# Feed-forward layers' last projections on one core: four weight blocks asked for one to two pairs sooner, all token parts in double tiles, neighbourhood steps regrouped

## The chip, the cores and the metric

The kernel runs on one core of a Trainium2 chip: TensorE (PE, matmuls), VectorE (DVE), ScalarE (ACT), GpSimd (POOL), SyncE (SP, which issues most loads) and 16 DMA engines. The metric is the device time of one execution in microseconds (us), the lower the better.

## The reference

One layer for 512 tokens of width 1024 in float32: a feed-forward layer (FFN1), a mixer of two attention branches, and a second feed-forward layer (FFN2), each between RMS norms.

```python
def _swiglu(x, w_gate, w_up, w_down):
    return (jax.nn.silu(x @ w_gate) * (x @ w_up)) @ w_down      # w_gate, w_up: 1024 x 2816, w_down: 2816 x 1024
...
f = _swiglu(_rmsnorm(x, ffn1_pre_g[l]), ffn1_w_gate[l], ffn1_w_up[l], ffn1_w_down[l])
x = x + 0.5 * _rmsnorm(f, ffn1_post_g[l])
h = _rmsnorm(x, mix_pre_g[l])
proj = h @ w_in[l]                                              # 1024 x 5888
...
ya = _neighbourhood_attention(qa, ka, va, na_rpb[l]) @ w_branch_a[l]   # 8 heads of 64, an 8 x 16 neighbourhood
yb = _dilated_mixture(qb, kb, vb, slopes) @ w_branch_b[l]
merged = jax.nn.sigmoid(gate_a) * ya + jax.nn.sigmoid(gate_b) * yb
x = x + _rmsnorm(merged @ w_out[l], mix_post_g[l])
# and f, x once more with the weights of ffn2
```

## The kernel before

**Numbers in two parts.** Every float32 operand is split into a high part (a cast by ACT, L116) and a low part (a subtraction by DVE, L117); a product is three matmuls into one bank: high by high, high by low, low by high (`mm3`, L207 to L209). PE takes both parts of both operands, so a product waits for ACT and, for its third matmul at the latest, for DVE's low parts.

**Seven products.** The matrices of the feed-forward layers are cut into two by two blocks and multiplied with seven products instead of eight (numbered 1 to 7), which need sums and differences of blocks. Sums of weight blocks are made by accumulating DMAs, issued by POOL (a second block is added on top of a loaded one while it is moved), or by DVE; differences of token parts (`v`) by DVE.

**The last projection** (`down`, class `Blocks`). The hidden features stand in units; its weight blocks are 128 x 1024 each, `((i, j), d)` for i, j in 0, 1 and d = 0 to 4, and one narrower row `EXTRA`. `order` is the list of (product, d) that PE runs through: (2,0), (2,1), then product 1 for all d, 5, 6, the rest of 2, 7, then 3 and 4. `prep` makes what one of them needs: the token part (`tokens`, its split into `a` or `pair`) and the weight block (`rows`, its split into `w`), `AHEAD` = 6 places before PE's `run`. Product 1 takes block (0,0) as loaded; product 5 takes it after block (0,1) was added by DMA (`t1`), product 6 that plus block (1,1) (`t2`: by DMA for d = 2 to 4 (L724), by DVE at L774 for d = 0 and 1).

**Places in memory.** A unit is 128 x 512 (`unit`, 38 of them, shared by nearly everything). `ta`, `tb`, `ba`, `bb` are larger places, each for two blocks, that were parts of the normalised tokens `hn`; they come free only when PE has read `hn` for the last time. Of the blocks (0,0) and (1,1), d = 0 to 3 go to `ta`, `tb` and `ba`, `bb`, and d = 4 into units, in two halves (`rows`, L731). A token part's high and low part are either two units (`a`) or one double tile (`pair`, 8 of them, `twin`); `o.paired` says which parts get a double tile: from the ninth on every third.

**When loads are asked for.** During the last pairs of the first projections (`seven`, 20 pairs of block columns) the function `get(j)` runs two pairs ahead; where no pair is left to load it calls the next list of `far`, and `ready` the next list of `lead`: a table of loads (`ld`) and preparations (`pr`) of the last projection. `later` holds loads by the place in `order`.

**The mixer.** Steps of the neighbourhood attention are strewn between projections: `sc` the scores of two heads, `tr` the transposes of one head's probabilities (PE, L1159, split by ACT and DVE into `pair`), `pv` their product with the values (L1186). `plan[p]` lists groups of steps; one group is run after each stretch of a projection.

**Order.** On each engine a scheduler sets the order from its own estimates of durations; some stretches are fixed to the order of the program, SP's first half among them.

Of the kernel before, what the change touches and what calls it, by code (L numbers as in the profile page):

```python
# [16 lines left out]
ALU = mybir.AluOpType  # L17
# [22 lines left out]
AHEAD = 6  # L40
# [6 lines left out]
def block_kernel(ctx, tc, x, gains, weights, rpb_near, rpb_all, alibi0, alibi12, out):  # L47
    nc = tc.nc
# [12 lines left out]
    def unit(dt=F32, name="u"):  # L61
        return up.tile([P, 512], dt, tag="u", name=name)
# [86 lines left out]
    def by_dma(n):  # L149


        hi, lo = [[unit(F32R, "w"), unit(F32R, "w")] for _ in range(2)]
        for i, cs in enumerate(halves):
            nc.gpsimd.dma_start(hi[i], weights[n][:, cs])
        yield
        for i in range(2):
            nc.scalar.mul(lo[i], hi[i].bitcast(F32), -1.0)
        for i, cs in enumerate(halves):
            nc.gpsimd.dma_start(lo[i], weights[n][:, cs], accum_op=ALU.add)
        pieces[n] = (hi, lo)  # L160
        yield
# [29 lines left out]
    def mark():  # L191
        return len(nc.cur_bb.bb.instructions)
# [232 lines left out]
    def seven(use, mv, n_pairs, n0, behind, far, lead, raws, early, put, pin):  # L425
# [6 lines left out]
        o = {}  # L432

        def get(j):
            if j < n_pairs and j > 2:
                raws[j] = load_blocks(n0, j)
            elif j >= n_pairs:
                behind(far)

        def ready(j, i):  # L440
# [40 lines left out]
        for j in range(n_pairs + 1):  # L481
            now, was = j < n_pairs, j > 0
            get(j + 2)
            if now:
# [7 lines left out]
                u = unit(name="up")  # L492
# [46 lines left out]
    def first_of_next():  # L539
        return [n for n in sorted(spread) if n >= state["next"]][:SPREAD]  # L540
# [139 lines left out]
    def parts_of(raw):  # L680

        return zip(raw, halves) if isinstance(raw, list) else [(raw, slice(0, PIECE))]
# [3 lines left out]
    class Blocks:  # L686
# [80 lines left out]
        def rows(self, i, d):  # L767
            raw = self.raw
            if i == 6:
                if ("t2", d) in raw:  # L770
                    return raw["t2", d]
                t = raw["t2", d] = raw.pop(("t1", d))
                assert not isinstance(t, list)
                nc.vector.tensor_tensor(t, t, raw[(1, 1), d], op=ALU.add)  # L774
                return t
            if i == 5:
                return raw["t1", d]
            if i == 1:
                return raw[(0, 0), d]
            return raw.pop({2: ((1, 0), d), 3: ((1, 1), d), 7: ("t3", d), 4: ("t4", d)}[i])  # L780
# [53 lines left out]
    def down(m, n0, duos, hidden, g_post, g_pre, store, src):  # L834

        o = Blocks(n0, m // 2, duos)
        sub, add = ALU.subtract, ALU.add

        nd, last = m // 2, m // 2 - 2
        after = {(1, EXTRA): ("r", "q", add), (6, EXTRA): ("c", "q", sub)}  # L840

        def each(i, lo=0):
            return [*((i, d) for d in range(lo, nd)), (i, EXTRA)]

        seq = [(2, 0), (2, 1), *each(1), *each(5), *each(6), *each(2, 2), *each(7), (3, 0)]

        seq += [(3, EXTRA), (3, 1), (4, 0), (4, 1), (4, EXTRA)] if store else [(3, 1), (4, 0), (4, 1)]
        tail = range(nd - last, nd)
        ks = list(tail) + [EXTRA] * (not store)
        order = seq + [(3, d) for d in tail] + [(4, d) for d in tail]  # L850
        o.paired = order[AHEAD + 2::3]
        ld = lambda *at: lambda: o.load(*at)
        pr = lambda n: lambda: o.prep(*order[n])
        far = deque([[ld(((1, 0), 0), "u"), ld(((1, 0), 1), "u")], [], []])
        home = lambda d, names: (names[d // 2], d % 2) if d < 4 else ("u", names)
        a_of, b_of = [lambda d, names=names: home(d, names) for names in (("ta", "tb"), ("ba", "bb"))]
        first = lambda d: ld(((0, 0), d), *a_of(d))
        lead = deque([
            [first(0)], [first(1), pr(0)], [first(2)], [first(3), pr(1)], [first(d) for d in range(4, nd)],
            [pr(2), ld(("t1", 0))], [], [pr(3), ld(("t1", 1))], [], [pr(4), ld(("t1", 2))], [], [pr(5), ld(("t1", 3))],  # L860
            [], []])
        later = {0: [ld(("t1", d)) for d in range(4, nd)] + [ld(((1, 1), d), *b_of(d)) for d in (0, 1)],
                 1: [ld(((1, 1), d), *b_of(d)) for d in range(2, nd)], 3: [ld(((1, 0), 2))], 4: [ld(((1, 0), 3))],
                 9: [ld(((1, 0), d), "u") for d in range(4, nd)]}

        def add_later(i, of, key, wait=0):
            for d in range(nd):
                later.setdefault(order.index((i, d)) - AHEAD + wait, []).append(ld((key, d), *of(d)))

        for d in BYDMA[:nd - 2]:  # L870
            later.setdefault(order.index((5, d)) - AHEAD, []).append(ld(("t2", d)))
        add_later(6, lambda d: (), "t3")
        add_later(7, b_of, (1, 1))
        add_later(6, lambda d: (), "t4", 8)

        lead[4].append(ld(((0, 0), EXTRA)))
        for n, f in ((1, ("t1", EXTRA)), (3, ((1, 1), EXTRA)), (order.index((5, EXTRA)) - AHEAD, ("t2", EXTRA)),
                     (5, ("t3", EXTRA)), (9, ((1, 0), EXTRA)), (order.index((6, EXTRA)) - AHEAD + 3, ("t4", EXTRA)),
                     (order.index((7, EXTRA)) - AHEAD, ((1, 1), EXTRA))):
            later.setdefault(n, []).append(ld(f))  # L880
        for i in (3, 4) if not store else ():
            later.setdefault(len(seq) - 10 + 2 * i, []).append(lambda i=i: o.prep(i, EXTRA))

        def rest():
            o.single = [hidden[2 * m + k] for k in range(2)]
            early = [] if store else [by_dma(n) for n in first_of_next()] * 2
            way_out = mark()
            for n, s in enumerate(seq):
                if store and n == len(seq) - 2:

                    nc.gpsimd.drain()
                if n + AHEAD < len(order):
                    o.prep(*order[n + AHEAD])
                for f in later.get(n, ()):
                    f()
                if n >= len(seq) - len(early):
                    next(early[n - len(seq)])
                o.run(*s)
                if s == (5, EXTRA):

                    o.acc["z"] = [o.part("c", t) for t in range(2)]
                elif s == (7, EXTRA):
                    with tc.high_priority(offset=URGENT):
                        for z, q in zip(o.acc["z"], o.acc["q"]):
                            nc.vector.tensor_tensor(z, z, q, op=sub)
                elif s in after:
                    o.onto(*after[s])
            state["take"] = n0 + 2 * m + 2
            state["used"] = True
            if not store:  # L910
                state["next"] = n0 + 2 * m + 2 + SPREAD
            acc1 = o.acc["c"] + o.acc["z"]

            def one(t, d):
                o.run(4 if t > 1 else 3, d, (t % 2,))

            def ends(t, b):
                return ks[-1] if b == (t < 2) else None

            rows_out((o.acc["r"] + o.acc["q"], acc1), ks, (None, ks[0], ks[1], ks[1]), one, ends, g_post, 4.0, g_pre, store, src)  # L920
            pool.append((way_out, mark(), (mybir.EngineType.Pool,)))

        return far, lead, rest
# [322 lines left out]
    def mixing(g):  # L1246
# [48 lines left out]
        def na_use(p, pq, pk):  # L1295
            if p < 3:
                load_tables(na_tab[p + 1], 3, bias_f[:, (p + 1) * 1536:(p + 2) * 1536])
            parts = qk_parts("na", pq, pk)
            sc = lambda: na_sc(parts, 2 * p)
            plan = (((sc,), (), ((na_tr, 0),)),  # L1300
                    (((na_tr, 1),), (sc,), ((na_pv, 0),), ((na_pv, 1), (na_tr, 2))),
                    (((na_tr, 3),), (sc,)),
                    (((na_pv, 2),), ((na_pv, 3), (na_tr, 4)), ((na_tr, 5),), (sc,), ((na_pv, 4),),
                     ((na_pv, 5), (na_tr, 6)), ((na_tr, 7),), ((na_pv, 6), (na_pv, 7))))
            for group in plan[p]:
                pend.append(lambda group=group: [f() if callable(f) else f[0](f[1]) for f in group])

# [97 lines left out]
        o = Blocks(n0, 1, duos)  # L1405
# [32 lines left out]
        order = [(2, 0), (1, 0), ("z", 4, 1), (5, 0), (6, 0), ("r", 4, 0), (7, 0), (3, 0), ("w", 6, 0), ("w", 6, 1), (4, 0)]  # L1438
# [60 lines left out]
        for n, s in enumerate(seq):  # L1499
            if len(s) == 2:  # L1500
                o.run(*s)
            else:
                for key in s[0]:
                    first = o.open(key)
# [51 lines left out]
    for n in range(2, 4):  # L1556
        raw = wp.tile([P, PIECE], F32, tag="raw", name="raw", bufs=2)
# [25 lines left out]
    first, second = row_half(0), row_half(1)  # L1583
# [207 lines left out]
```

## Time and profile before

| | us |
|---|---|
| median of three runs | 1081.47 (1080.14 to 1081.65) |
| the profiled execution | 1083.46 |
| its span, first to last instruction | 1081.7 |
| PE busy, share of the span | 1068.9, 99% |
| DVE busy | 862.3, 80% |
| ACT busy | 656.1, 61% |
| POOL busy | 179.1, 17% |
| bytes by DMA | 193.98 MB, 179 GB/s on average |

The granted PE clock was 0.997 over the span. FFN1's last projection ends at about 337 us of the span, FFN2's with the span. Matmuls overlap one another, so their durations add up to more than their time: PE's losses are read from the distances between the starts. `[4.50 <-DMA ba<-...]` behind a row says that the engine stood idle for 4.50 us before it and what ended that.

### The profile page before, as it was taken

Reading aid. Unit: us, or ns where it says so; the run is one execution under the profiler, and the core shown is the slowest. Engines: PE = TensorE matmul, PEld = TensorE weight load, DVE = VectorE, ACT = ScalarE, POOL = GpSimd, SP = SyncE. Lnnn points to the kernel's source line nnn. Section 1 sums busy time; section 2 is a strip of 40 time slices with the busy share of each in tenths; the row PEclk is TensorE's granted clock in tenths of the full one; section 3 lists DMA queues with packets and bytes.
Section 4 is the critical chain, followed back from the end, with each engine's and each line's share of the span. In section 5 each row is a group of like instructions: output and inputs, shape, how many; then the busy total and the mean of one; then the engine's idle time right before and its main releaser. Section 6 shows DMA issues by size and latency. Waiting matters only on the chain.

```text
span 1081.7 us, 17625 instructions
## 1 busy us (share of the span) xinstructions
PE 1068.9 (99%) x6211; PEld 939.4 (87%) x6211; DVE 862.3 (80%) x1652; ACT 656.1 (61%) x1340; POOL 179.1 (17%) x247
## 2 busy tenths in 40 slices
PE   9999999999999999999999999999999999999997
PEld 7899999998788988888988888889899999987786
DVE  7988988878897666676777644777999898888995
ACT  7655666565594665567766641376656666675681
POOL 4111121024234000000000001143301111114201
PEclk9999999999999999999999999999999999999999
DMA  9989988579996454322222239586937777769962
GB/s 333 193 215 225 230 201 216 151 183 266 247 237 187 148 183 151 114 77 79 80 87 96 78 113 303 151 199 202 280 83 194 180 181 192 201 186 222 227 203 78
DMA packets 98027, 193.98 MB, mean 179 GB/s; under 512 B 24337, under 2 KB 26897, under 8 KB 97938
## 3 DMA queue, kind: packets, MB, share of 16 engines
q1 hardware_dynamic: 70624, 138.37, 37.9%
q0 software_dynamic: 24624, 54.01, 28.2%
q8 instruction: 49, 0.80, 0.3%
q10 hardware_dynamic: 2690, 0.46, 0.2%
q14 instruction: 40, 0.33, 0.1%
HBM read 185.68 MB, written 9.68 MB: 181 GB/s over the span
## 4 chain that ended last, share of the span: by engine, by line
PE 92%; DVE 3%; DMA 2%; ACT 2%; issue 1%; POOL 0%; SPq 0%; DVEq 0%; ACTq 0%; POOLq 0%
PE ps L207 9%; PE ps L209 9%; PE ps L208 9%; PE q L209 8%; PE q L207 8%; PE q L208 8%; PE p L458 6%; PE q L458 5%; PE p L460 3%; PE r L208 3%; PE r L209 3%; PE r L207 3%; PE q L460 2%; PE c L207 2%; PE c L208 2%; PE c L209 1%
## 5 line engine op out<-in xcount | busy, mean ns | idle before, releaser
L117 DVE TENSOR_TENSOR w<-raw,w 128x512 fp32r<-128x512 f32 (+1 forms) x138 | 125.1, 911 | 78.4 <-ACT w L116 77.2
L116 ACT CAST w<-raw 128x512 fp32r<-128x512 f32 (+1 forms) x138 | 109.7, 802 | 89.9 <-PE ps L208 32.5
L207 PE MATMUL ps<-hn,w 128*128 128x512 f32 (+1 forms) x360 | 136.5, 379 | 0.0
L209 PE MATMUL ps<-hn,w 128*128 128x512 f32 (+1 forms) x360 | 134.5, 374 | 0.0
L208 PE MATMUL ps<-hn,w 128*128 128x512 f32 (+1 forms) x360 | 134.3, 373 | 0.0
L116 ACT CAST w<-t 128x512 fp32r<-128x512 f32 x160 | 97.2, 621 | 58.7 <-DVE t L413 32.1
L117 DVE TENSOR_TENSOR w<-t,w 128x512 fp32r<-128x512 f32 x160 | 107.6, 685 | 4.8 <-ACT w L116 4.4
L458 PE MATMUL p<-v,w 128*128 128x512 f32 x256 | 93.2, 398 | 0.0
L407 POOL DMA_DIRECT2D t<-in_weights_dram x40 | 35.0, 874 | 289.9 <-DVE w L117 85.1
L458 PE MATMUL q<-v,w 128*128 128x512 f32 x224 | 81.6, 397 | 0.0
L208 PE MATMUL q<-hn,w 128*128 128x256 f32 x288 | 81.4, 283 | 0.0
L209 PE MATMUL q<-hn,w 128*128 128x256 f32 x288 | 81.4, 283 | 0.0
L207 PE MATMUL q<-hn,w 128*128 128x256 f32 x288 | 81.2, 283 | 0.0
L209 PEld LDWEIGHTS ps<-hn,w 128*128 128x128 f32 x360 | 67.8, 188 | 12.7 <-DVE w L117 0.7
L207 PEld LDWEIGHTS ps<-hn,w 128*128 128x128 f32 x360 | 67.9, 189 | 11.5
L208 PEld LDWEIGHTS ps<-hn,w 128*128 128x128 f32 x360 | 67.9, 189 | 10.9
L460 PE MATMUL p<-v,w 128*128 128x256 f32 x256 | 71.1, 281 | 0.0
L460 PE MATMUL q<-v,w 128*128 128x256 f32 x224 | 62.9, 281 | 0.0
L207 PE MATMUL q<-w,a 128*128 128x512 f32 x156 | 61.4, 394 | 0.5 <-ACT a L116 0.5
L209 PE MATMUL q<-w,a 128*128 128x512 f32 x156 | 59.7, 395 | 1.7 <-DVE a L117 1.6
L208 PE MATMUL q<-w,a 128*128 128x512 f32 x156 | 61.2, 392 | 0.0
L207 PEld LDWEIGHTS q<-hn,w 128*128 128x128 f32 x288 | 54.6, 190 | 1.8
(345 smaller groups left out, 3067.2 us busy)
## 6 DMA issues: line engine op xcount, KB each, us to landing
raw<-in_weights_dram SPq DMA_DIRECT2D x90, 512.0 KB
t<-in_weights_dram SPq DMA_DIRECT2D x88, 256.0 KB
t<-in_weights_dram POOLq DMA_DIRECT2D x80, 256.0 KB, 5.6
w<-in_weights_dram SPq DMA_DIRECT2D x40, 256.0 KB
rows<-in_weights_dram SPq DMA_DIRECT2D x32, 256.0 KB
w<-in_weights_dram POOLq DMA_DIRECT2D x32, 256.0 KB, 6.0
tb<-in_weights_dram POOLq DMA_DIRECT2D x12, 512.0 KB, 7.4
rows<-in_weights_dram POOLq DMA_DIRECT2D x24, 256.0 KB, 10.4
```

The costliest lines, as they stand in the source:

```text
L116: nc.scalar.copy(hi, src)
L117: nc.vector.tensor_tensor(lo, src, hi.bitcast(F32), op=ALU.subtract)
L207: nc.tensor.matmul(o, sh, mh, start=start, stop=False, **kw)
L208: nc.tensor.matmul(o, sh, ml, start=False, stop=False, **kw)
L209: nc.tensor.matmul(o, sl, mh, start=False, stop=stop, **kw)
L407: nc.gpsimd.dma_start(t1, weights[gate][:, :512], accum_op=ALU.add)
L458: nc.tensor.matmul(o[key, j], w[:, k * P:(k + 1) * P], mv[i][k][2], start=start and k == 0, stop=False, skip_group_check=True)
L460: nc.tensor.matmul(acc, w[:, 512 + k * P:512 + (k + 1) * P], mv[i][k][0], start=False, stop=k == 3, skip_group_check=True)
```

## The change

Three things are changed. First, `far` begins one pair sooner (`j >= n_pairs - 1`) and has a list more: blocks (0,0) with d = 0 and 1 are loaded there, into units; d = 2, 3 and 4 follow in `lead` into `ta` and half of `tb`, two places sooner than they were; block (1,1) with d = 4 goes into the other half of `tb`. With that, blocks 0 and 1 come in halves of 512 wherever they are split, added (L774, which becomes L775) or loaded, and block 4 in whole tiles. Second, all token parts from the ninth on use double tiles. Third, the last list of the neighbourhood's `plan` puts its steps into other groups.

```diff
             if j < n_pairs and j > 2:
                 raws[j] = load_blocks(n0, j)
-            elif j >= n_pairs:
+            if j >= n_pairs - 1:
                 behind(far)
...
                 t = raw["t2", d] = raw.pop(("t1", d))
-                assert not isinstance(t, list)
-                nc.vector.tensor_tensor(t, t, raw[(1, 1), d], op=ALU.add)
+                b = raw[(1, 1), d]
+                for u, cs in parts_of(t):
+                    nc.vector.tensor_tensor(u, u, b[:, cs], op=ALU.add)
                 return t
...
-        o.paired = order[AHEAD + 2::3]
+        o.paired = order[AHEAD + 2:]
         ld = lambda *at: lambda: o.load(*at)
         pr = lambda n: lambda: o.prep(*order[n])
-        far = deque([[ld(((1, 0), 0), "u"), ld(((1, 0), 1), "u")], [], []])
-        home = lambda d, names: (names[d // 2], d % 2) if d < 4 else ("u", names)
-        a_of, b_of = [lambda d, names=names: home(d, names) for names in (("ta", "tb"), ("ba", "bb"))]
+        a_of = lambda d: ("u", d) if d < 2 else ("ta", d - 2) if d < 4 else ("tb", 0)
+        b_of = lambda d: (("ba", "bb")[d // 2], d % 2) if d < 4 else ("tb", 1)
         first = lambda d: ld(((0, 0), d), *a_of(d))
+        far = deque([[first(0), first(1)], [ld(((1, 0), 0), "u"), ld(((1, 0), 1), "u")], [], []])
         lead = deque([
-            [first(0)], [first(1), pr(0)], [first(2)], [first(3), pr(1)], [first(d) for d in range(4, nd)],
+            [first(2)], [first(3), pr(0)], [first(4)], [pr(1)], [],
             [pr(2), ld(("t1", 0))], [], [pr(3), ld(("t1", 1))], [], [pr(4), ld(("t1", 2))], [], [pr(5), ld(("t1", 3))],
             [], []])
...
                     (((na_tr, 3),), (sc,)),
-                    (((na_pv, 2),), ((na_pv, 3), (na_tr, 4)), ((na_tr, 5),), (sc,), ((na_pv, 4),),
-                     ((na_pv, 5), (na_tr, 6)), ((na_tr, 7),), ((na_pv, 6), (na_pv, 7))))
+                    (((na_pv, 2),), ((na_pv, 3), (na_tr, 4)), (sc,), ((na_pv, 4), (na_tr, 5)), ((na_pv, 5),),
+                     ((na_tr, 6),), ((na_pv, 6), (na_tr, 7)), ((na_pv, 7),)))
```

What it does to the order on the engines is shown at three places. The first is SP's queue in FFN1, from the last pair's weights (`w11`) to the loads of `ba`. Before, `rows_2898` to `rows_2903` are block (1,0) with d = 0 and 1, `rows_3126` and `rows_3127` block (0,0) with d = 4:

```order
L406 DMA w11_2762<-in_weights_dram 128x512
L731 DMA rows_2898<-in_weights_dram 128x512
L731 DMA rows_2899<-in_weights_dram 128x512
L731 DMA rows_2902<-in_weights_dram 128x512
L731 DMA rows_2903<-in_weights_dram 128x512
L735 DMA ta_3046<-in_weights_dram 128x1024 x2
L735 DMA tb_3086<-in_weights_dram 128x1024 x2
L731 DMA rows_3126<-in_weights_dram 128x512
L731 DMA rows_3127<-in_weights_dram 128x512
L718 DMA rows_3130<-in_weights_dram 128x512
L735 DMA ba_3240<-in_weights_dram 128x1024 x2
```

Now, with `rows_2772` to `rows_2777` for block (0,0), d = 0 and 1, and `rows_2906` to `rows_2911` for block (1,0):

```order
L406 DMA w11_2762<-in_weights_dram 128x512
L731 DMA rows_2772<-in_weights_dram 128x512
L731 DMA rows_2773<-in_weights_dram 128x512
L731 DMA rows_2776<-in_weights_dram 128x512
L731 DMA rows_2777<-in_weights_dram 128x512
L731 DMA rows_2906<-in_weights_dram 128x512
L731 DMA rows_2907<-in_weights_dram 128x512
L731 DMA rows_2910<-in_weights_dram 128x512
L731 DMA rows_2911<-in_weights_dram 128x512
L735 DMA ta_3054<-in_weights_dram 128x1024 x2
L735 DMA tb_3094<-in_weights_dram 128x1024
L718 DMA rows_3133<-in_weights_dram 128x512
```

Block (0,0) with d = 0 and 1 moved ahead of (1,0), and behind `ta` there is a load of 512 KB and two of 256 KB less.

The second is DVE's queue in FFN1 around the low half of the token part for product 6, block 1, which PE waits for before the change: `a_3453`, and afterwards `pair_3456`. Before:

```order
L117 TENSOR_TENSOR w_3507<-tb_3086,w_3506 128x1024
L832 TENSOR_TENSOR r_3243<-r_3243,part_3421 128x512
L832 TENSOR_TENSOR r_3244<-r_3244,part_3424 128x512
L764 TENSOR_TENSOR v_3406<-v_3406,h_584 128x256
L117 TENSOR_TENSOR w_3529<-rows_3126,w_3528 128x512
L117 TENSOR_TENSOR w_3529<-rows_3127,w_3528 128x512
L117 TENSOR_TENSOR a_3453<-v_3306,a_3452 128x512
```

Now:

```order
L117 TENSOR_TENSOR w_3435<-rows_2772,w_3434 128x512
L117 TENSOR_TENSOR w_3435<-rows_2773,w_3434 128x512
L833 TENSOR_TENSOR r_3249<-r_3249,part_3422 128x512
L833 TENSOR_TENSOR r_3250<-r_3250,part_3425 128x512
L117 TENSOR_TENSOR pair_3456<-v_3311,pair_3456 128x512
L764 TENSOR_TENSOR v_3362<-v_3362,h_1571 128x512
L764 TENSOR_TENSOR v_3385<-v_3385,h_1833 128x512
L117 TENSOR_TENSOR w_3462<-rows_2776,w_3461 128x512
```

Before, the part stands behind weights of product 6, blocks 3 and 4 (`w_3507`, `w_3529`); now it stands ahead of the weights of its own block (`w_3462`).

The third is DVE's queue in FFN2 from the additions of `ba` (L774, L775) to the token part of product 5, block 2: `a_11217` before, `pair_11208` now. Before:

```order
L774 TENSOR_TENSOR ta_10941<-ta_10941,ba_11122 128x1024
L117 TENSOR_TENSOR w_11221<-tb_10975,w_11220 128x1024
L764 TENSOR_TENSOR v_11165<-v_11165,h_8853 128x512
L117 TENSOR_TENSOR a_11191<-v_11188,a_11190 128x512
L764 TENSOR_TENSOR v_11214<-h_9297,h_10537 128x512
L774 TENSOR_TENSOR ta_10941<-ta_10941,ba_11122 128x1024
L117 TENSOR_TENSOR w_11245<-tb_10975,w_11244 128x1024
L764 TENSOR_TENSOR v_11188<-v_11188,h_9046 128x512
L117 TENSOR_TENSOR w_11269<-rows_11011,w_11268 128x512
L117 TENSOR_TENSOR w_11269<-rows_11012,w_11268 128x512
L117 TENSOR_TENSOR a_11217<-v_11214,a_11216 128x512
```

Now, behind the additions (two halves for block 0, an L632 of 256 elements, the split of `pair_11156`, two halves for block 1):

```order
L117 TENSOR_TENSOR w_11212<-ta_10935,w_11211 128x1024
L764 TENSOR_TENSOR v_11206<-h_9283,h_10523 128x512
L117 TENSOR_TENSOR pair_11181<-v_11179,pair_11181 128x512
L764 TENSOR_TENSOR v_11230<-h_9531,h_10779 128x512
L764 TENSOR_TENSOR v_11253<-h_9779,h_11023 128x512
L764 TENSOR_TENSOR v_11154<-v_11154,h_8839 128x512
L117 TENSOR_TENSOR w_11236<-ta_10935,w_11235 128x1024
L764 TENSOR_TENSOR v_11275<-h_8626,h_8689 128x256
L117 TENSOR_TENSOR w_11259<-tb_10969,w_11258 128x1024
L764 TENSOR_TENSOR v_11179<-v_11179,h_9032 128x512
L117 TENSOR_TENSOR w_11280<-rows_11004,w_11280 128x512
L117 TENSOR_TENSOR pair_11208<-v_11206,pair_11208 128x512
```

The part stood ten rows behind the first addition and now stands seventeen behind it.

## The prediction, made before the changed kernel had run

> **What bounds the kernel.** I read the page's busy table first, then PE's waits, then the timelines around them and the windows.
>
> ```profile
> span 1081.7 us, 17625 instructions
> PE 1068.9 (99%) x6211; PEld 939.4 (87%) x6211; DVE 862.3 (80%) x1652; ACT 656.1 (61%) x1340; POOL 179.1 (17%) x247
> ...
> PE q L209 <- DVE a L117: 1.6, 1, 1.6
> ...
> PE c L209 <- DVE pair L117: 1.1, 1, 1.1
> ```
>
> PE is the bound, and no instruction of PE is added or taken away. So the change can only win what PE loses waiting, and the two longest single waits, and nearly all of the rest, lie in the last projections. Their true size is read from starts (PE's timeline; columns: start, duration, instruction, idle before and releaser):
>
> ```profile
> 273.43 0.39 PE L207 MATMUL q<-w,a 128*128 128x512 f32 x1
> 273.65 0.39 PE L208 MATMUL q<-w,a 128*128 128x512 f32 x1
> 274.05 1.00 PE L207 MATMUL r<-w,pair 128*128 128x512 f32 x2
> 276.69 0.50 PE L209 MATMUL q<-w,a 128*128 128x512 f32 x1 [1.64 <-DVE a L117]
> ...
> 336.67 0.39 PE L209 MATMUL q<-w,pair 128*128 128x512 f32 x1
> 337.48 0.66 PE L342 MATMUL ps<-ident,u 128*128 128x128 f32 x4 [0.42 <-DVE u L323]
> ...
> 996.45 0.39 PE L208 MATMUL c<-w,pair 128*128 128x512 f32 x1
> 997.98 0.50 PE L209 MATMUL c<-w,pair 128*128 128x512 f32 x1 [1.14 <-DVE pair L117]
> ...
> 1007.63 0.39 PE L207 MATMUL r<-w,pair 128*128 128x512 f32 x1
> 1008.68 0.49 PE L207 MATMUL r<-w,pair 128*128 128x512 f32 x1 [0.66 <-DVE r L832]
> ...
> 276.69:280.30 3.61, 3.61 (x9) 2.82 (x10) 2.80 (x4) 0.58 (x1) 2.10 (x4) 0.56 1.05 232
> ```
>
> Back to back, 128x512 matmuls start 0.22 us apart (273.43 to 273.65; over longer runs 0.227). *First projection (FFN1)*: between 273.65 and 276.69 stand three starts worth 0.68, so 2.36 are lost. Then the clock falls: the last row (a window; after the five busy columns come granted clock, DMA share, GB/s) gives 0.56 and nine matmuls in 3.61 us, worth 2.04: 1.57 lost. With some tenths on either side of it, about 4.4 us. *Turn to the mixer*: 336.67 to 337.48, less 0.23: 0.6. *Second projection (FFN2)*: 996.45 to 997.98 less 0.23 is 1.3; 1007.63 to 1008.68 less 0.23 is 0.8; with smaller gaps until 1012 about 3.5. Together 8.5 us can be won at most.
>
> Why PE waits there is told by DVE and, behind it, the loads (DVE's, then SP's timeline):
>
> ```profile
> 249.67 1.23 DVE L774 TENSOR_TENSOR ta<-ta,ba 128x1024 f32<-128x1024 f32 x1 [4.50 <-DMA ba<-in_weights_dram]
> ...
> 252.55 0.69 DVE L117 TENSOR_TENSOR a<-v,a 128x512 fp32r<-128x512 f32 x1
> 253.15 1.22 DVE L774 TENSOR_TENSOR ta<-ta,ba 128x1024 f32<-128x1024 f32 x1
> 254.28 1.22 DVE L117 TENSOR_TENSOR w<-tb,w 128x1024 fp32r<-128x1024 f32 x1
> ...
> 275.94 0.69 DVE L117 TENSOR_TENSOR a<-v,a 128x512 fp32r<-128x512 f32 x1
> ...
> 980.55 0.69 DVE L117 TENSOR_TENSOR pair<-v,pair 128x512 fp32r<-128x512 f32 x1
> 984.92 1.23 DVE L774 TENSOR_TENSOR ta<-ta,ba 128x1024 f32<-128x1024 f32 x1 [3.68 <-DMA ba<-in_weights_dram]
> ...
> 201.44 2.75 SPq L731 DMA_DIRECT2D rows<-in_weights_dram  x4
> 223.06 0.80 SPq L735 DMA_DIRECT2D ta<-in_weights_dram  x2
> ...
> 241.17 0.88 SPq L735 DMA_DIRECT2D ba<-in_weights_dram  x2
> ...
> 938.89 2.19 SPq L731 DMA_DIRECT2D rows<-in_weights_dram  x4
> ...
> 973.68 1.20 SPq L731 DMA_DIRECT2D rows<-in_weights_dram  x2
> 976.36 1.87 SPq L735 DMA_DIRECT2D ba<-in_weights_dram  x2
> ...
> 225.00:230.00 5.00, 5.00 (x44) 5.00 (x43) 2.90 (x6) 3.29 (x6) 0.69 (x1) 1.00 1.01 410
> ...
> 215.00:220.00 5.00, 5.00 (x44) 5.00 (x44) 4.28 (x9) 2.77 (x6) 0.00 (x0) 1.00 0.01 3
> 945.00:950.00 5.00, 5.00 (x36) 4.63 (x35) 5.00 (x11) 2.63 (x7) 0.00 (x0) 1.00 0.10 39
> 958.00:990.00 32.00, 32.00 (x166) 27.42 (x166) 25.50 (x39) 19.24 (x31) 6.94 (x8) 1.00 0.99 266
> ```
>
> DVE stands 4.50 and 3.68 us for the block `ba`, asked for at 241.17 and 976.36 and landed 8.5 us later, because the DMA engines are full (share 1.01, 0.99), while just before (215 to 220, 945 to 950) they stood nearly empty (0.01, 0.10). After that wait DVE works without a pause until PE has caught it, and PE waits for a token part that DVE wrote at 275.94.
>
> **The change part by part.**
>
> *Four blocks sooner, two in units.* 1 MB of plain loads, `(0,0)` blocks 0 and 1, goes from SP's place at 223 to that at 201.44 (FFN1), in FFN2 to that at 938.89, some 17 us sooner: from the full stretch to where the empty one takes up what follows. At the 410 GB/s of the quoted window 1 MB is 2.6 us of DMA time. SP issues four 256 KB loads more in front of `(1,0)`, and whole tiles fewer at 223; these places wait for units whose last readers are over by then, as those of the four `rows` loads were that stand there now. Block 4 of `(1,1)` goes into `tb` behind `bb`, so the two loads at 973.68 no longer stand ahead of `ba`: 0.5 MB, 1.25 us.
>
> *Halves.* Blocks 0 and 1 are split and added as two of 512 for one of 1024. Next instruction starts 0.60 us after a 512 (252.55 to 253.15) and 1.13 after a 1024 (253.15 to 254.28): 0.07 us more for each of some eight, 0.6 in all per FFN, less what block 4 saves as whole tiles. DVE hides it where it has slack; in FFN2 it lies in the queue that I add up below. Their additions on the DMA queue become pieces of 256 KB:
>
> ```profile
> rows<-in_weights_dram POOLq DMA_DIRECT2D x24, 256.0 KB, 10.4
> ...
> ta<-in_weights_dram POOLq DMA_DIRECT2D x8, 512.0 KB, 10.9
> ```
>
> Two pieces together may take between 0 and 10 us longer than one of 512 KB; since the bytes are the same, I take the near end, 0. They are asked for some 12 us before the split that needs them.
>
> *Double tiles for all parts.* Before, two parts in three lived in units, and a unit came free only when PE was through with old parts; so DVE's late part (275.94) stood behind both `r` additions and the weights of two later blocks. Now it stands behind the `r` additions and ahead of those weights. Adding the queue from the first `ba` addition at an unchanged 249.67: 14 instructions of 512 (8.4), two of 1024 (2.3), two of 256 (0.33 each, 0.7) end at 261.0, where PE asks at about 274.4. The tightest part of that stretch keeps some 1 us. So the FFN1 stall goes, and its clock fall with it: -4.4 (bounds -4.4 and 0). What is late next there is the block-3 part, by the 1 us named.
>
> *FFN2* is different: both additions of `ba` still stand ahead of the part for product 5, block 2 (`pair_11208`), and seven rows more than before. From 984.92: 13 of 512 (7.8), three of 1024 (3.4), two of 256 (0.7) end at 996.8; PE asks for it at 994.4, where it meets that block today. So an unmoved `ba` costs 2.4 us, no longer 3.5 spread over four waits. DVE is free for the addition at about 981.2 (980.55 plus 0.69), so each us that `ba` lands sooner takes one off, up to 3.7. I take 1.25 (the two loads gone) and leave the 1 MB aside, since its turn is long over by 976: left 1.2, which did not lower the clock today (1.3 at 996.45, matmuls at 0.23 behind it). FFN2 -2.3; bounds -3.5 (all gone) and +0.5 (2.4 and a clock fall of 1.6).
>
> The Trainium skill, "DMA: Bandwidth & Descriptors", Queues, rings and completion order, says that each DMA engine takes packets in turn from the rings it has work for. By that rule the hardware ring gets half while additions run, 0.5 MB ahead of `ba` is 2.5 us, and the rest would be 0 in place of 1.2; no row here separates the two rings' shares.
>
> *The turn at 337.* The loads of `x` wait for units freed late:
>
> ```profile
> 324.96 6.60 SPq L70 DMA_DIRECT2D x<-in_x_dram  x8
> ...
> 331.41 1.30 DVE L117 TENSOR_TENSOR w<-rows,w 128x512 fp32r<-128x512 f32 x2 [2.34 <-ACT w L116]
> ...
> 333.22 1.41 DVE L604 SCALAR_TENSOR_TENSOR x<-u,rstd,x 128x512 f32<-128x512 f32 x2
> ```
>
> They are asked for earlier now, and the last weight split moves behind L604 on DVE, which otherwise waits for ACT until 331.41. Gain 0 to 0.6; I take 0.6, as both things ahead of L604 move.
>
> *Neighbourhood steps.* Four probabilities' transposes now have only one run of 24 projection matmuls (24 x 0.227 = 5.4 us) before the product that reads them. PE lost nothing here:
>
> ```profile
> 440.00:495.00 55.00, 55.00 (x298) 46.78 (x298) 39.47 (x87) 34.18 (x76) 0.00 (x0) 1.00 0.31 99
> ...
> 483.58 1.03 PE L1159 MATMUL ps<-ident,u 128*128 128x128 f32 x8
> ...
> 487.49 0.69 DVE L117 TENSOR_TENSOR pair<-ps,pair 128x512 fp32r<-128x512 f32 x1
> ```
>
> From the end of the transposes (484.6) to the end of their second split (488.2) are 3.6 us, under 5.4. So 0, between -0.2 and +0.6 each.
>
> *Sum.* -4.4 - 2.3 - 0.6 = -7.3; for new small waits of the size seen above (0.66 at 1008.68) I add one of 0.6: -6.7. The profiled execution took 1083.46 (span 1081.7 and 1.8 around it), hence 1076.8; it lies 2.0 above the median of the runs, 1081.47, against which this makes **1074.8**.
>
> **Rivals.**
>
> *A: FFN2 keeps its stall.* `ba` lands at 984.9 as before, because additions and not plain loads set its pace (958 to 990 is full at 266 GB/s). The wait of 2.4 is as long as the 2.36 after which the clock fell, so 1.6 more: +0.5 for FFN2, and -4.4 - 0.6 + 0.5 + 0.6 = -3.9, 1077.6. Against it: two loads do stand ahead of `ba` today.
> The Trainium skill, "TensorE: Matmul & The Clock Gate", Part 1, has the clock fall only after an idle window of about 3.4 us. By it A would end at 1076.0; the quoted row at 0.56 behind 2.36 us disagrees, so I give the rule little.
>
> *B: the stall only changes its place*, within 0.2%. If the two 256 KB pieces land 3 us later in FFN1, the additions of `ba` slip 3 us, the 1 us of margin is gone, and a stall of 2 with its clock fall (1.6) stands where 4.4 stood; with A's FFN2 that is -4.4 + 3.6 + 0.5 - 0.6 + 0.6 = -0.3, 1081.2. For it: pieces of 256 KB already take 10.4. Against it: 12 us of lead.
>
> *C: slower, by the neighbourhood.* If DVE, 39.47 of 55 us busy there, gets to the splits later than in today's 3.6 us, PE stands at each of four products. Against a gain of 6.7 it decides from (6.7 + 2.2) / 4 = 2.2 us each, that is from a delay of 7.6 us, twice today's. At 9 us: 4 x 3.6 = 14.4, and 1081.47 - 6.7 + 14.4 = 1089.
>
> *D: the change does nothing*: the DMA engines stay the limit, and DVE's wait for `ba` only begins sooner: 1081. Against it: the part PE waits for has 13 us of margin in the new queue.
>
> **How the numbers follow.** Forecast 0.52 (its own range 1072.5 to 1076.5); A 0.27; B 0.10; D 0.04; C 0.07. 0.2% (2.2 us) is about what a measurement of this kernel tells from no change. Faster: forecast and A, 0.79; within: B and D, 0.14; slower: C, 0.07. Low end: all 8.5, and the neighbourhood's -0.2 twice, 1072.5 (rounded). High end 1079: A with four products of +0.3 each; beyond it lie B, D and C.
>
> **What would show it.** Right: PE without a wait between 266 and 281 and clock 1.00 there; one wait of 0 to 1.5 us on a `pair` in FFN2; `ba` some 1.3 us sooner there; `x` loads before 320; no wait of PE on the neighbourhood's `pair`. Wrong: a window with clock near 0.5 in either projection, or PE waiting for DVE's `pair<-ps` at four places.

## The result, and the profile after

The changed kernel takes 1075.65 us (median of six runs, 1074.42 to 1076.83) against 1081.65 (median of five) for the kernel before in the same series. The ratio is 0.994, 95% interval 0.9928 to 0.9952, so 6.5 us less (5.2 to 7.8); the medians alone differ by 6.0. Forecast were 1074.8, within 1072.5 to 1079. The profiled execution took 1076.83. Here and below, single executions that took far longer (1309 to 3760 us, of several kernels, the one before among them) are left out of medians and ratios.

The page of the changed kernel, and PE's waits in it (columns: in total, times, longest):

```profile
span 1075.0 us, 17610 instructions
PE 1065.4 (99%) x6211; PEld 938.9 (87%) x6211; DVE 862.0 (80%) x1660; ACT 657.4 (61%) x1344; POOL 184.7 (17%) x247
...
PE warm L1569 <- DVE idle L1533: 1.2, 1, 1.2
PE q L207 <- ACT part L827: 1.0, 1, 1.0
PE c L209 <- DVE pair L117: 0.6, 1, 0.6
```

The busy time of each engine is the same within 6 us; what is shorter is the waiting. The waits of 1.6 on a part in units and of 0.4 at L342 are off the list; two waits are left in FFN2 (the one on `warm` is at the start and was there before). The places that the prediction named, by windows and by PE's and DVE's timelines:

```profile
276.69:280.30 3.61, 3.61 (x18) 2.99 (x17) 3.61 (x6) 1.16 (x3) 3.41 (x4) 1.00 1.07 212
266.00:281.00 15.00, 15.00 (x68) 12.43 (x67) 15.00 (x23) 9.39 (x17) 5.47 (x7) 1.00 1.08 227
...
332.45 0.39 PE L209 MATMUL q<-w,pair 128*128 128x512 f32 x1
332.68 1.03 PE L342 MATMUL ps<-ident,u 128*128 128x128 f32 x8
...
988.02 0.39 PE L208 MATMUL c<-w,pair 128*128 128x512 f32 x1
989.44 0.98 PE L207 MATMUL q<-w,pair 128*128 128x512 f32 x2 [1.04 <-ACT part L827]
991.02 0.50 PE L209 MATMUL c<-w,pair 128*128 128x512 f32 x1 [0.60 <-DVE pair L117]
...
440.00:495.00 55.00, 55.00 (x311) 46.49 (x310) 39.05 (x82) 33.28 (x67) 0.00 (x0) 1.00 0.25 77
```

In the window where nine matmuls ran at a clock of 0.56 there are now eighteen at 1.00. The turn to the mixer follows the last product by 0.23 us, without a gap. FFN2 still loses 1.2 (988.02 to 989.44, less 0.23) and 1.1 (989.44 to 991.02, less two starts), 2.3 together. The neighbourhood is as free of waits as before. From the starts of all matmuls: FFN1's stall -4.3, the turn -0.6 with its smaller neighbours -1.0, FFN2 3.7 to 2.5, some tenths elsewhere: the 6.7 us that the span is shorter.

Where the loads stand now (SP's timeline, DVE's additions of `ba`, POOL's additions by DMA in FFN2):

```profile
199.90 8.89 SPq L731 DMA_DIRECT2D rows<-in_weights_dram  x8
...
241.34 0.80 SPq L735 DMA_DIRECT2D ba<-in_weights_dram  x2
...
970.38 1.19 SPq L735 DMA_DIRECT2D ba<-in_weights_dram  x2
...
245.75 0.69 DVE L775 TENSOR_TENSOR rows<-rows,ba 128x512 f32<-128x512 f32 x1
...
978.97 1.29 DVE L775 TENSOR_TENSOR rows<-rows,ba 128x512 f32<-128x512 f32 x2 [4.12 <-DMA ba<-in_weights_dram]
...
241.10 0.88 POOL L724 DMA_DIRECT2D tb<-in_weights_dram  x1 [2.08 <-DVE w L117]
...
968.23 0.87 POOL L724 DMA_DIRECT2D tb<-in_weights_dram  x1 [1.21 <-DVE w L117]
970.03 0.87 POOL L724 DMA_DIRECT2D rows<-in_weights_dram  x1 [0.94 <-DVE w L117]
```

The eight loads of 256 KB at 199.90 take SP 8.9 us, since some wait for their units (SP's waits name DVE's `w` and `h` as what they wait for), and are still over before the next request at 223. In FFN1 `ba` is there 4.4 us after its request or sooner, DVE does not wait, and the wait of 4.50 is gone. In FFN2 it still takes 8.6 us (970.38 to 978.97), as before (976.36 to 984.92), though 1.5 MB of the plain loads ahead of it are asked for some 17 us sooner. A difference between the two places is in the last rows: in FFN1 the addition into `tb` was asked for 0.24 us ahead of `ba`, in FFN2 2.15 us.

### The profile page after: what moved, and what is told of

The parts are those of the page before. It is cut to its first block, busy times and chain, and to the rows that moved or that the text cites. A ratio compares the mean times of both kernels' runs of the same rounds, so it can differ in the third digit from the quotient of the medians.

```text
span 1075.0 us, 17610 instructions
## 1 busy us (share of the span) xinstructions
PE 1065.4 (99%) x6211; PEld 938.9 (87%) x6211; DVE 862.0 (80%) x1660; ACT 657.4 (61%) x1344; POOL 184.7 (17%) x247
## 4 chain that ended last, share of the span: by engine, by line
PE 97%; DVE 1%; DMA 1%; issue 0%; ACT 0%; DVEq 0%; ACTq 0%
PE ps L207 11%; PE ps L209 11%; PE ps L208 10%; PE q L208 8%; PE q L209 8%; PE q L207 8%; PE p L458 6%; PE q L458 5%; PE p L460 3%; PE r L209 3%; PE r L208 3%; PE r L207 3%; PE q L460 2%; PE c L209 2%; PE c L207 2%; PE c L208 2%
## 5 line engine op out<-in xcount | busy, mean ns | idle before, releaser
L209 PE MATMUL ps<-hn,w 128*128 128x512 f32 (+1 forms) x360 | 134.6, 374 | 0.0
L209 PE MATMUL q<-hn,w 128*128 128x256 f32 x288 | 81.4, 283 | 0.0
L209 PEld LDWEIGHTS ps<-hn,w 128*128 128x128 f32 x360 | 67.8, 188 | 12.7 <-DVE w L117 0.7
L207 PEld LDWEIGHTS q<-hn,w 128*128 128x128 f32 x288 | 54.6, 190 | 1.8
L458 PEld LDWEIGHTS p<-v,w 128*128 128x128 f32 x256 | 48.0, 188 | 8.9
L743 POOL DMA_DIRECT2D rb<-in_weights_dram x3 | 2.7, 894 | 306.1 <-DMA rb<-in_weights_dram 305.9
L208 PEld LDWEIGHTS q<-hn,w 128*128 128x128 f32 x288 | 54.7, 190 | 0.6
```

The lines of the kernel that those rows point to most:

```text
L207: nc.tensor.matmul(o, sh, mh, start=start, stop=False, **kw)
L208: nc.tensor.matmul(o, sh, ml, start=False, stop=False, **kw)
L209: nc.tensor.matmul(o, sl, mh, start=False, stop=stop, **kw)
L458: nc.tensor.matmul(o[key, j], w[:, k * P:(k + 1) * P], mv[i][k][2], start=start and k == 0, stop=False, skip_group_check=True)
L743: nc.gpsimd.dma_start(to, self.block(*b, 0), accum_op=ALU.add)
```

## The experiments

Each ratio is to the kernel before, timed on the same chip, with its 95% interval. Two theories stood at the start. *The queue*: FFN1's stall came of token parts in units, placed behind later weights on DVE. *The loads*: DVE was only late because it stood 4.5 us for `ba`.

**e1, the loads alone.** Of the diff all but these two lines:

```diff
-        o.paired = order[AHEAD + 2:]
+        o.paired = order[AHEAD + 2::3]
```
and the neighbourhood's `plan` as before.

> Before with the sooner loads alone (blocks 0 and 1 in units, block 4 in whole tiles); double tiles and neighbourhood groups as before. Theory 1, the DVE queue: the FFN1 stall came of token parts in units that stood behind later weights, so it stays in part: 1079 to 1081, with a wait of PE on a DVE low part near 270 and a clock fall. Rival 2, the loads: DVE was late only because it stood 4.5 us for ba, so the loads alone bring most of the gain: 1076 to 1077, with ba in FFN1 some 4 us after its request and no stall at 274.

1077.46 us, ratio 0.9972 (0.9963 to 0.9981): about half the gain, between the two theories' ranges. PE's longest wait, and DVE's addition in FFN1:

```profile
PE c L209 <- DVE pair L117: 1.8, 1, 1.8
...
245.23 0.68 DVE L775 TENSOR_TENSOR rows<-rows,ba 128x512 f32<-128x512 f32 x1
```

FFN1's stall is gone without the double tiles, which the queue theory denied. What is left is FFN2: 1.9 at 990.8 and about 1.1 after it, near the 3.5 it was.

**e2, the double tiles alone.**

```diff
-        o.paired = order[AHEAD + 2::3]
+        o.paired = order[AHEAD + 2:]
```

> Before with the double tiles for all parts alone. Theory 1: the FFN1 stall goes, although DVE still stands some 4 us for ba: 1076.5 to 1078. Rival 2: ba still lands 8.5 us after its request, DVE is as late as before and PE stalls as before: 1080.5 to 1082.

1078.03, ratio 0.998 (0.9967 to 0.9992). Both stalls of before are gone, in FFN1 and at 996 in FFN2, although DVE still waits for `ba` in both:

```profile
973.88 2.31 SPq L735 DMA_DIRECT2D ba<-in_weights_dram  x2
...
248.54 1.23 DVE L774 TENSOR_TENSOR ta<-ta,ba 128x1024 f32<-128x1024 f32 x1 [3.24 <-DMA ba<-in_weights_dram]
...
982.49 1.22 DVE L774 TENSOR_TENSOR ta<-ta,ba 128x1024 f32<-128x1024 f32 x1 [3.73 <-DMA ba<-in_weights_dram]
...
309.86 0.63 ACT L157 ACTIVATE w<-w 128x512 fp32r<-128x512 f32 x1 [5.58 <-DMA w<-in_weights_dram]
...
314.29 1.04 ACT L116 CAST w<-bb 128x1024 fp32r<-128x1024 f32 x1
...
317.93 0.47 PE L207 MATMUL q<-w,pair 128*128 128x512 f32 x1 [2.85 <-ACT w L116]
```

So the loads theory falls too, as the only cause: either remedy alone is enough for FFN1's stall, since DVE has to be late and PE's part has to stand behind other work. (That `ba` came 1.1 us sooner here than in the profile of before is not the reason: in e3 below, with the old tiles, DVE adds it at the same moment and PE stalls.) In FFN2 `ba` lands 8.6 us after its request (973.88 to 982.49), as late as before, and PE loses nothing near it; there the loads alone (e1) removed little, the double tiles alone everything.

But a new stall of 3.0 has come at 314.7: the double tiles free units, the mixer's first weights are fetched into them by POOL some 14 us sooner (first request 289.79 in place of 303.37), and ACT's step on them (L157) now stands ahead of the weights of FFN1's last products and waits 5.58 us for its DMA. In the whole change the same step waits too, but PE does not feel it:

```profile
307.94 0.63 ACT L157 ACTIVATE w<-w 128x512 fp32r<-128x512 f32 x1 [3.35 <-DMA w<-in_weights_dram]
...
311.35 1.03 ACT L116 CAST w<-bb 128x1024 fp32r<-128x1024 f32 x1
```

**e3 and e4, the neighbourhood steps alone, and the change without them.**

```diff
-                    (((na_pv, 2),), ((na_pv, 3), (na_tr, 4)), ((na_tr, 5),), (sc,), ((na_pv, 4),),
-                     ((na_pv, 5), (na_tr, 6)), ((na_tr, 7),), ((na_pv, 6), (na_pv, 7))))
+                    (((na_pv, 2),), ((na_pv, 3), (na_tr, 4)), (sc,), ((na_pv, 4), (na_tr, 5)), ((na_pv, 5),),
+                     ((na_tr, 6),), ((na_pv, 6), (na_tr, 7)), ((na_pv, 7),)))
```
(e4 has these lines the other way round.)

> Before with the regrouped neighbourhood steps alone. The trace of after shows no wait of PE there, so 0 to -0.6 us against before (1081 to 1082). A rival, that the regrouping carries a part of the gain, asks for 2 us or more.

> The change without the regrouped neighbourhood steps: if they carry nothing, 1075.5 to 1076.3, as the whole change (1075.65); if they carry a part, above 1077.

e3: 1081.61, ratio 1.0008 (0.9999 to 1.0017). e4: 1074.98, ratio 0.995 (0.9937 to 0.9963). The regrouping carries none of the gain. The feed-forward layers of e3 are those of before, so its trace is also a second look at FFN1's stall:

```profile
248.74 1.23 DVE L774 TENSOR_TENSOR ta<-ta,ba 128x1024 f32<-128x1024 f32 x1 [3.31 <-DMA ba<-in_weights_dram]
...
275.75 0.50 PE L209 MATMUL q<-w,a 128*128 128x512 f32 x1 [1.34 <-DVE a L117]
...
275.75:279.20 3.45, 3.45 (x15) 2.83 (x16) 3.45 (x5) 0.62 (x1) 1.92 (x4) 1.00 1.06 230
```

`ba` landed 7.3 us after its request, the wait was shorter than the 1.64 of before, and the clock stayed at 1.00 behind it. How large the stall is differs from one execution to the next.

**e5 and e7, `ba` sooner.** The first loads of `ba` become units, asked for behind block (1,0), and the addition at L775 takes them as halves (not shown); e7 is the same with the old neighbourhood groups.

```diff
-        far = deque([[first(0), first(1)], [ld(((1, 0), 0), "u"), ld(((1, 0), 1), "u")], [], []])
+        far = deque([[first(0), first(1)], [ld(((1, 0), 0), "u"), ld(((1, 0), 1), "u")], [ld(((1, 1), 0), "u")], [ld(((1, 1), 1), "u")]])
...
-        later = {0: [ld(("t1", d)) for d in range(4, nd)] + [ld(((1, 1), d), *b_of(d)) for d in (0, 1)],
+        later = {0: [ld(("t1", d)) for d in range(4, nd)],
```

> The whole change, and block (1,1) with d = 0 and 1 asked for in the same empty stretch, into units, in place of the first loads of ba. If DVE's 4 us wait for ba is the root of what FFN2 still loses (2.3 us in the trace of after): no such wait, PE's losses between 980 and 1000 under 0.5 us, 1073.2 to 1074.2 against 1075.65. Rival: the order of DVE's queue or the ACT queue holds PE in FFN2, ba is hidden: 1075 to 1076.5.

> As the kernel with block (1,1) sooner, with the neighbourhood steps grouped as before the change: 0.3 to 0.7 below that kernel, if the small loss seen with the regrouping alone is real; the same within 0.3 if not.

1084.73, ratio 1.0027 (1.0015 to 1.0039), and 1083.72, 1.0025 (1.0015 to 1.0036): slower than the kernel before, which neither side expected. DVE's wait for `ba` is indeed gone, but PE (e5's waits, timeline and a window) stands elsewhere, once in each projection:

```profile
PE c L207 <- ACT a L116: 5.3, 2, 3.1
PE q L207 <- ACT part L828: 1.2, 1, 1.2
...
270.80 0.50 PE L207 MATMUL c<-w,a 128*128 128x512 f32 x1 [2.12 <-ACT a L116]
...
1000.73 0.40 ACT L116 CAST a<-v 128x256 fp32r<-128x256 f32 x1
...
1001.18 0.50 PE L207 MATMUL c<-w,a 128*128 128x512 f32 x1 [3.14 <-ACT a L116]
...
1005.00:1010.00 5.00, 5.00 (x14) 3.93 (x13) 4.50 (x10) 0.99 (x2) 2.85 (x4) 0.53 1.10 204
```

On ACT in FFN2 the cast of the part for product 5, `EXTRA`, now stands behind six later weights and eight later parts, and some of those weights wait for tiles that PE frees only as it proceeds. That the scheduler did this because it reckoned with an early `ba` is a guess. The clock falls to 0.53 behind the waits in FFN2. So this run says nothing against `ba` as the root; it shows what a moved load does through the order. e7 shows the same waits, and as a test of the neighbourhood it decides nothing.

**e6, two additions later.** The requests of `t1` for blocks 3 and 4 move behind that of `ba` in the program, in FFN2 alone:

```diff
-            [pr(2), ld(("t1", 0))], [], [pr(3), ld(("t1", 1))], [], [pr(4), ld(("t1", 2))], [], [pr(5), ld(("t1", 3))],
+            [pr(2), ld(("t1", 0))], [], [pr(3), ld(("t1", 1))], [], [pr(4), ld(("t1", 2))], [], [pr(5)] + [ld(("t1", 3))] * (not store),
...
-        later = {0: [ld(("t1", d)) for d in range(4, nd)] + [ld(((1, 1), d), *b_of(d)) for d in (0, 1)],
-                 1: [ld(((1, 1), d), *b_of(d)) for d in range(2, nd)],
+        later = {0: [ld(("t1", d)) for d in range(4, nd)] * (not store) + [ld(((1, 1), d), *b_of(d)) for d in (0, 1)],
+                 1: [ld(((1, 1), d), *b_of(d)) for d in range(2, nd)] + [ld(("t1", 3))] * store,
+                 2: [ld(("t1", 4))] * store,
```

> The whole change, and in FFN2 the additions t1 of blocks 3 and 4 asked for one to two places later, so that fewer additions stand on the DMA engines when ba is asked for. If additions set when ba lands: it lands 4 to 6 us after its request, as in FFN1 of after (4.4), in place of 8.6, and DVE's wait falls from 4.1 to some 1: 1074 to 1075, unless blocks 3 and 4 come late in their turn. Rival: plain loads set it: 8 to 9 us, wait and time as in after.

1074.86, ratio 0.9938 (0.9925 to 0.995). In the trace the one addition into `tb` that stood 2.15 us ahead of `ba` now stands 0.18 behind it; the other additions and `ba` itself are asked for as before:

```profile
970.19 0.80 SPq L735 DMA_DIRECT2D ba<-in_weights_dram  x2
...
970.37 1.22 POOL L724 DMA_DIRECT2D tb<-in_weights_dram  x1
...
975.22 1.29 DVE L775 TENSOR_TENSOR rows<-rows,ba 128x512 f32<-128x512 f32 x2 [0.57 <-DMA ba<-in_weights_dram]
...
979.54 1.29 DVE L775 TENSOR_TENSOR rows<-rows,ba 128x512 f32<-128x512 f32 x2 [2.09 <-DMA ba<-in_weights_dram]
...
988.06 0.80 PE L207 MATMUL q<-w,pair 128*128 128x512 f32 x2
988.85 0.50 PE L209 MATMUL c<-w,pair 128*128 128x512 f32 x1
```

The first of the two loads of `ba` lands 5.0 us after the request in place of 8.6, and DVE waits 0.57 for it. For the second load, which the change had without a further wait, DVE now waits another 2.09, so 2.66 in all in place of 4.12. PE loses 0.3 (988.06 to 988.85, less two starts) in place of 2.3. In the time of the whole this is not to be seen: the ratio is that of the change within the intervals.

**e9 and e10, the additions later without the neighbourhood's regrouping, and the whole change again,** on one chip.

> The whole change with the two additions of FFN2 later, and the neighbourhood steps grouped as before the change: if their regrouping costs 0.3, as its run alone and the run without it say, 0.3 to 0.6 below the kernel with the additions later (1074.86): 1074.2 to 1074.6. If not, the same.

> The whole change once more, on the chip of these runs, to set the two against: 1075.0 to 1076.5.

1075.34, ratio 0.9947 (0.9931 to 0.9962), and 1076.06, 0.9953 (0.9939 to 0.9968). The expected 0.3 below e6 is not there by the ratios (0.9947 and 0.9938, intervals that overlap), so the times leave open whether the regrouping costs anything. The traces show no cost: from the turn to the mixer to the start of product 5 in FFN2, PE takes 649.2 us in the change, e6 and e10 (with it) and in e4 and e9 (without). In its trace e9 has no wait of PE in FFN2 left. e10 is worth a look for another reason:

```profile
969.99 1.14 SPq L735 DMA_DIRECT2D ba<-in_weights_dram  x2
...
976.61 1.29 DVE L775 TENSOR_TENSOR rows<-rows,ba 128x512 f32<-128x512 f32 x2 [2.15 <-DMA ba<-in_weights_dram]
...
979.02 1.29 DVE L775 TENSOR_TENSOR rows<-rows,ba 128x512 f32<-128x512 f32 x2 [0.18 <-DMA ba<-in_weights_dram]
```

The same kernel, and the first load of `ba` lands after 6.6 us instead of 8.6. Over five traces that share this stretch, but for the place of the one addition in e6 and e9, time from request to landing and PE's loss at 988 go together: 8.6 and 2.3 (the change), 7.6 and 1.1 (e4), 6.6 and 0.6 (e10), 5.0 and 0.3 (e6), 5.1 and 0.1 (e9). The second load tells less: DVE starts on it 9.0 us after the request in e10 and 9.4 in e6, so moving the addition did not bring the whole of `ba` sooner than this execution of the change had it.

**e8 and e11, whether the loads of `x` hold up ACT in e2.** e2, with the loads of all token groups but the first inside the loop that finishes the groups; in the trace those of the last two come later.

```diff
-            for t in range(NT):
+            for t in range(1 if pin else NT):
                 load_x(t, src)
...
         for t in range(NT):
+            if src is not None and pin and t < NT - 1:
+                load_x(t + 1, src)
```

> The double tiles alone, with the loads of x for the last two of the four token groups asked for only as the group before is finished (1 MB later; the double tiles had freed units for them some 20 us sooner, at 305 us). If these loads hold up the mixer's first weights on the DMA engines, for which ACT stood 5.6 us at 309.9 with the weights of the last products behind it: ACT's wait there falls to some 3, PE's 3.0 us at 314.7 to under 1, 1075.5 to 1076.5 against 1078.1. Rival: another load or order holds ACT: 1077.5 to 1078.5.

> A second look at the double tiles with the last x loads later, for the profile of an undisturbed run. Its time, 1078.5 against 1078.1 with the x loads early, speaks against them: then ACT still stands over 4 us for the mixer's weights near 310 and PE some 3 us behind it. If ACT's wait is gone, another stall has taken its place elsewhere.

e8: 1078.43, ratio 0.9973 (0.9964 to 0.9982), as e2. The second look (e11, one execution, 1080.05):

```profile
306.46 9.45 SPq L70 DMA_DIRECT2D x<-in_x_dram  x4
...
309.81 0.63 ACT L157 ACTIVATE w<-w 128x512 fp32r<-128x512 f32 x1 [4.38 <-DMA w<-in_weights_dram]
...
318.13 0.76 PE L207 MATMUL q<-w,pair 128*128 128x512 f32 x1 [3.26 <-ACT w L116]
```

Half of the `x` loads are gone from that place, and still ACT gets the mixer's weights at the same moment (309.81 and 309.86) and PE loses 3.4 us: the guess that `x` crowds out the mixer's weights is wrong. That the order on ACT puts L157 ahead is seen; why its weights come so late in e2 (POOL asks for them one by one, each behind a wait of 1.8 to 3.5 us) and whether that alone makes the 3 us, no run settles.

## Why the prediction was right

*FFN1's stall* (-4.4): -4.3 between the two profiles, and no clock fall. The working gave the queue the whole credit; e1 and e2 show that either half of the change removes it. The term came out right because both were in it, not because the double tiles were needed for it. That the loads sooner would also bring `ba` sooner in FFN1 I left out; it came 4 us sooner than in the profile of before (3 us against e2 and e3), more than the 2.6 us of DMA time of the 1 MB. The 4.4 itself was one execution's: in e3 the same stall and its smaller neighbours cost 2.9, without a clock fall.

*FFN2* (-2.3, from 3.5 to 1.2): in the profiled run from 3.5 to 2.3, so a term mis-sized by 1.1. The step was `ba` 1.25 us sooner, for two loads of 256 KB no longer ahead of it; in that trace it took 8.6 us as before. In e4 and e10 it took 1.0 and 1.9 less, so the size was within the spread, but the reason is not shown: the two loads were away in all three executions. What stands ahead of it counts in another way: with one addition of 512 KB moved from 2 us ahead to just behind (e6, e9), the first load of `ba` lands 1.6 to 3.6 us sooner than in the three. The other part of the step, the queue of DVE behind `ba`, was right for the new order: an unmoved `ba` was to cost 2.4 and cost 2.3, and at 7.6 and 6.6 us the loss fell to 1.1 and 0.6 where the working gives 1.4 and 0.5. (A little luck is in the 2.4: it has PE asking at 994.4, where in the trace of before PE reached that block's low part, the row `c<-w,a` of L209, at 993.83; the two matmuls named below made up for it.) It was not the whole cause of FFN2's stall, though: e2 has `ba` as late and loses nothing there, e1 has the sooner loads and loses 3. The gain in FFN2 came with the double tiles, and what the change still loses came with the order that the sooner loads made; which rows of that order do it, no run separates.

*Rival A* had its landing (8.6) and not its price: no clock fall followed. The order on PE puts two matmuls of product 6 into the wait, which broke it into 1.2 and 1.1; that this is why the clock held is not shown.

The Trainium skill's "DMA: Bandwidth & Descriptors", Queues, rings and completion order, has each DMA engine take packets in turn from the rings it has work for. By the prediction's reckoning from that rule FFN2 was to lose nothing. The profiled run's 8.6 speaks against that reckoning, and e6's 5.0 goes with an addition that stands elsewhere; how the rings share is still not seen.

On the clock, the prediction took the fall behind 2.36 lost us as what a wait of that length brings. The runs do not sort that way. PE's waits and the windows behind them, in this order: e1 after its wait of 1.8, e7, e5 after its wait of 2.12, e2 after its wait of 2.85, e11 after its wait of 3.26:

```profile
992.93:996.54 3.61, 3.60 (x16) 3.00 (x17) 3.61 (x6) 0.89 (x2) 1.59 (x2) 1.00 1.06 203
...
270.62 0.50 PE L207 MATMUL c<-w,a 128*128 128x512 f32 x1 [1.89 <-ACT a L116]
270.62:274.23 3.61, 3.61 (x10) 2.85 (x11) 3.61 (x6) 0.43 (x1) 0.00 (x0) 0.60 1.08 213
...
270.80:274.41 3.61, 3.61 (x16) 3.00 (x17) 3.61 (x7) 0.42 (x1) 0.00 (x0) 1.00 1.10 217
...
317.93:321.54 3.61, 3.61 (x16) 2.98 (x17) 3.61 (x6) 3.61 (x9) 2.72 (x4) 1.00 1.07 256
...
318.13:321.74 3.61, 3.61 (x10) 2.91 (x11) 3.61 (x6) 3.61 (x9) 2.72 (x4) 0.59 1.09 254
```

A wait of 1.89 (and the 1.64 of before) was followed by a fall, one of 2.12 at the same place and one of 2.85 were not, one of 3.26 was. So the length of the wait alone does not decide between 1.6 and 2.9 us; what does, no run shows, and a clock fall should have been priced as a chance.

The Trainium skill's "TensorE: Matmul & The Clock Gate", Part 1, has a fall only after an idle window of about 3.4 us. The falls behind 1.64 and 1.89 disagree with it, as does e11's behind 3.26; e2's 2.85 without a fall agrees.

*The turn* (-0.6): -0.6, with the `x` loads asked for at 303 in place of 325. *The neighbourhood* (0): none in e3 within 0.2%. *New small waits* (+0.6): none of that size came outside FFN2. So FFN2 won 1.1 less than forecast and these waits cost 0.6 less, and the two misses partly cancel; with the 4.4 that was one execution's, some of the sum's nearness is luck. ACT's wait for the mixer's weights, which no part of the prediction named, stood ready to become one of 3 us, as e2 shows.

## What to carry to other kernels

Where an engine's stall has two conditions, a late producer and an unlucky place in its queue, removing either can be enough: here both halves cured FFN1's stall, and what set them apart was the wait that each left (FFN2 in e1) or made (ACT in e2). A stall read from one execution is one draw: look at a second before pricing it, a clock fall above all. A free buffer starts the next stage's loads and puts the engine work that waits for them ahead in its queue, so look at what the freed places start. And when a plain load lands late, look for the accumulating DMA asked for just ahead of it before counting megabytes.

## What the runs showed of the hardware

With one accumulating DMA of 512 KB asked for 2.15 us ahead of a plain 512 KB load, on nearly full DMA engines (share 0.92 from 952 to 984 in the change, 0.94 in e6), the load landed after 8.6, 7.6, 7.4 and 6.6 us (the change, e4, e1, e10). With that addition asked for 0.18 us behind it, it landed after 5.0 and 5.1 (e6, e9), but the second load of the pair then kept DVE waiting another 2.09 and 1.81. With 1.5 MB more of plain loads and other additions ahead of it, it took 8.6, 8.6 and 8.7 us (before, e2, e3). The spread of 2 us between executions of the same stretch was not expected: it is as large as what the kernel still loses there.

Waits of PE between 1.6 and 2.9 us were followed by a granted clock of 0.56 to 0.60 in some executions (1.64 before, 1.89 in e7) and of 1.00 in others (1.8 in e1, 2.12 in e5, 2.85 in e2).
